# An encoder trunk on one core: how the gate, shift and scale rows of the conditioning are summed and turned

## The chip, the cores and the metric

The kernel runs on one core of a Trainium2 chip. The metric is device time in microseconds (us) of one execution. Several executions are given as a median with the lowest and highest.

## What is computed

Two layers, each of three sub-layers: a SwiGLU feed-forward block, a token mixer, a second SwiGLU block. Each sub-layer is conditioned by nine rows of 1024 numbers for a layer, three for each sub-layer (shift, scale, gate), which come from one vector c:

```python
for layer in range(DEPTH):                       # 2
    mod = (silu(c) @ w_ada[layer] + b_ada[layer]).reshape(b, N_SUB, 3, 1, D_MODEL)
    u = modulate(x, mod[:, 0, 0], mod[:, 0, 1])  # standardize(x) * (1 + scale) + shift
    f = swiglu(u, w_ffn_in[layer, 0], w_ffn_out[layer, 0])
    x = layer_norm(ALPHA * x + 0.5 * (1 + mod[:, 0, 2]) * f, ln_g[layer, 0], ln_b[layer, 0])
    # the mixer with mod[:, 1, :] (gate without the 0.5), the second SwiGLU with mod[:, 2, :]
```

x has 256 tokens of 1024 features; SwiGLU has 2816 hidden features. Everything is float32. w_ada is 1024 x 9216 for a layer.

## The kernel before

Tokens stand in two tiles of 128 partitions. A weight arrives by DMA as fp32 in a raw tile, is cast to fp32r by ACT (the high part, tiles h..) and subtracted from the raw tile by VectorE (the low part, tiles l..). A product of fp32 accuracy is then three fp32r products into the same PSUM bank (mm3, lines 150 to 153): high with high, high with low, low with high. In the trace ob and oa are the first products of a SwiGLU block, acc the second ones; ocx, ovx, ozx, oqkx and accx are those of the mixer.

All weights, the rows of w_ada among them, are items of one planned list (plan, step, issue_loads): the loads are issued in list order by SP as raw tiles come free (9 of them), and casts and splits take tiles from a pool of 26 (wtile). A SwiGLU block of 256 hidden features works in two halves j: 48 ob products, then 12 acc products of the block before (6 in the last blocks), then the evaluation of the half; after each half flush() emits what stands in the list late.

The conditioning goes like this. For each of the rows, ada_step (lines 318 to 333) takes eight raw tiles of 128 x 1024 and adds each, times a column of silu(c), into an accumulator of 128 x 1024 on VectorE. When the last one is in, ada_post (lines 386 to 406) is put in the list late. What remains to be done there is the sum over the 128 partitions:

- For a gate (w == 2) two fp32 products with a matrix of ones (pg, line 394) give the sum over the partitions on every partition, 512 columns each, and VectorE turns them into the gate's tile gr (line 395).
- For a shift or a scale four fp32 products with 32 columns of ones (pr, lines 398 to 400) each sum a quarter of the row, 256 columns, into one group of 32 partitions (tile_position). ACT copies that to SBUF (cpy, traced as adc), and two fp32 products with sel4 as the moving operand (pm, line 405) turn it into 8 columns, to which mod_cols (lines 375 to 384) adds the bias. sel4 (line 208) is 128 x 4 and has a one at partition 32 j of column j.

The first sub-layer's shift and scale go another way (adh_step) and are not touched. Ten rows go through the shift and scale branch, six through the gate branch. In the first SwiGLU block of layer 0 these are the mixer's shift and scale, the first gate, and the shift of the third sub-layer; in mixer 0 its gate and the scale of the third sub-layer; and so on, always before their use.

PSUM has a pool of two banks for small results (mps): pr, pg, pm and the transposes of the mixer (py) take turns in it. VectorE and ACT keep the written order in the transitions between sub-layers (cross, in_order); elsewhere the framework orders the instructions when the program is built, by their order in the program and by what is ready; TensorE is bound to the written order at the start of the program alone.

Of the kernel before, what the change touches and what calls it, by code (L numbers as in the profile page):

```python
# [12 lines left out]
F32R = mybir.dt.float32r  # L13
# [3 lines left out]
ALU = mybir.AluOpType  # L17
# [3 lines left out]
P = 128  # L21
D = 1024
KT = D // P
# [43 lines left out]
def kernel(  # L67
# [44 lines left out]
    V, S, PE = Queue(nc.vector), Queue(nc.scalar), Queue(nc.tensor)  # L112
# [9 lines left out]
    cp = ctx.enter_context(tc.tile_pool(name="cp", bufs=1))  # L122
# [9 lines left out]
    def wtile(shape, name, dt=F32):  # L132
        return wp.tile([P] + list(shape), dt, tag="w", name=name)

    def mps(name):
        return pms.tile([P, 512], F32, tag="ms", name=name)
# [10 lines left out]
    def f(ap):  # L147
        return ap.bitcast(F32)
# [6 lines left out]
    def split(src, hi, lo):  # L155
        S.copy(hi, src)
        V.tensor_tensor(lo, src, f(hi), op=ALU.subtract)


    ident = cp.tile([P, P], F32, name="ident")  # L160
    make_identity(nc, ident)
    ones = cp.tile([P, P], F32, name="ones")
# [29 lines left out]
    def issue_loads(upto):  # L192
        while pos["load"] < min(upto, 2 * len(items)):
            n = pos["load"]
            i, h = divmod(n, 2)
            kind, key, src = items[i]
            if kind == "pair":
                half = src[h].rearrange("(k p) c -> p k c", p=P)
            else:
                half = src.rearrange("(h k p) c -> h p k c", h=2, p=P)[h]  # L200
            shape = {"cols": [4, BC], "pair": [4, BC], "adh": [2, 512]}.get(kind, [1, D])
            raw = rp.tile([P] + shape, F32, tag="raw", name=f"raw_{key}_{h}")
            nc.sync.dma_start(raw, half)
            raws[n] = raw[:, 0, :] if shape[0] == 1 else raw
            pos["load"] += 1


    sel4 = cp.tile([P, 4], F32, name="sel4")
# [2 lines left out]
    sel1 = cp.tile([P, 1], F32, name="sel_all")  # L211
    V.tensor_reduce(sel1, sel4, axis=AX.X, op=ALU.add)

    ADA = ("ada", "adh")

    def hi_step():
        n = pos["hi"]
        i, h = divmod(n, 2)
        kind, key, _ = items[i]
        if kind in ADA:  # L220
            return False
# [13 lines left out]
    def step(n=1):  # L235
        for _ in range(n):
# [5 lines left out]
            issue_loads(k + 1)  # L242
            if kind in ADA:
                pos["hi"] = max(pos["hi"], k + 1)
# [35 lines left out]
    brs, bcol = [], []  # L280
# [26 lines left out]
    mods, gates, adas = {}, {}, {}  # L307
# [10 lines left out]
    def ada_step(key, raw, k):  # L318
        l, ch, q = key
        kt = 2 * q + k  # L320
        s, w = divmod(ch, 3)
        if kt == 0:
            adas[l, ch] = wtile([D], f"ada{l}_{ch}")
            if w == 2:
                G.memset(adas[l, ch], 0.0)
                nc.sync.dma_start(adas[l, ch][0:1, :], b_ada[l, ch * D:(ch + 1) * D].unsqueeze(0))
        acc = adas[l, ch]
        if kt == 0 and w < 2:
            keep(V.tensor_scalar(acc, raw, cT[:, 0:1], None, op0=ALU.mult), "v")
        else:  # L330
            keep(V.scalar_tensor_tensor(acc, raw, cT[:, kt:kt + 1], acc, op0=ALU.mult, op1=ALU.add), "v")
        if kt == KT - 1:
            late.append(lambda: ada_post(l, s, w, adas.pop((l, ch))))
# [41 lines left out]
    def mod_cols(l, s, w, pp):  # L375
        ch = 3 * s + w
        if w == 0:
            mods[l, s] = sm.tile([P, 2, KT], F32, tag="mod", name=f"mod{l}_{s}", bufs=3)
        md = mods[l, s]
        bc = bcol[l][:, ch * KT:(ch + 1) * KT]  # L380
        if w == 0:
            V.tensor_tensor(md[:, 0, :], pp[:, :KT], bc, op=ALU.add)
        else:
            V.scalar_tensor_tensor(md[:, 1, :], pp[:, :KT], 1.0, bc, op0=ALU.add, op1=ALU.add)

    def ada_post(l, s, w, acc):
        ch = 3 * s + w
        if w == 2:
            gr = wtile([D], f"gate{l}_{s}")
            gates[l, s] = gr  # L390
            half = 1.0 if s == 1 else 0.5
            for h in range(2):
                pp = mps(f"pg{l}_{s}_{h}")
                PE.matmul(pp, lhsT=ones, rhs=acc[:, h * 512:(h + 1) * 512], start=True, stop=True)
                V.tensor_scalar(gr[:, h * 512:(h + 1) * 512], pp, 1.0, half, op0=ALU.add, op1=ALU.mult)
            return
        pr = mps(f"pr{l}_{ch}")
        for j in range(4):
            PE.matmul(pr[32 * j:32 * j + 32, 0:256], lhsT=ones[:, 0:32], rhs=acc[:, j * 256:(j + 1) * 256],
                      start=True, stop=True, tile_position=(0, 32 * j))  # L400
        cpy = wtile([256], f"adc{l}_{ch}")
        S.copy(cpy, pr[:, 0:256])
        pp = mps(f"pm{l}_{ch}")
        for k in range(2):
            PE.matmul(pp[:, k:8:2], lhsT=cpy[:, k * P:(k + 1) * P], rhs=sel4, start=True, stop=True)
        mod_cols(l, s, w, pp)


    HALF = (slice(0, 512), slice(512, 1024))
# [949 lines left out]
```

## Time and profile before

| | |
|---|---|
| median of 3 runs | 1091.83 us (1090.25 to 1091.99) |
| profiled execution | 1089.88 us |
| its span, first to last instruction | 1088.2 us |
| mean granted TensorE clock | 0.986 of full speed |
| TensorE busy | 1041.0 us, 96% |
| VectorE busy | 834.7 us, 77% |
| ACT busy | 551.4 us, 51% |

PE is TensorE (its matrix products), PEld its loading of weights, DVE VectorE, ACT ScalarE, POOL GpSimd, SP the engine that issues the loads. In the rows "out<-in" names the tiles written and read; of a matrix product the moving operand comes first and the stationary one second. Durations of TensorE overlap, so what a product adds to the stream is read from the distance of starts, not from the durations. An fp32 product has two records, an fp32r product and a transpose one. "idle before <-" tells what ended the idle time of that engine. All rows that helpers record have the same line, L105.

### The profile page before, as it was taken

What the parts mean: (1) busy time and instruction counts of PE and PEld (TensorE: products, weight loads), DVE (VectorE), ACT (ScalarE), POOL (GpSimd) and SP (SyncE); (2) the same over time, 40 slices, a digit from 0 to 9 for tenths busy, and PEclk for the clock granted to TensorE, in tenths of its full rate; (3) what the DMA queues carried; (4) which work ended last, traced back from release to release, by engine and by line L of the source; (5) the groups of instructions that cost most, each with busy time, mean ns of one, the idle gap of its engine ahead of it and who ended that gap; (6) DMA issues with size and microseconds to landing.
All of it is one profiled execution on the core that took longest, in us unless ns stands there. A gap on an engine that the chain in (4) does not pass through costs nothing.

```text
span 1088.2 us, 18866 instructions
## 1 busy us (share of the span) xinstructions
PE 1041.0 (96%) x7381; PEld 953.2 (88%) x7381; DVE 834.7 (77%) x1303; ACT 551.4 (51%) x940; POOL 53.0 (5%) x93
## 2 busy tenths in 40 slices
PE   4999999999997999999999999999999989999996
PEld 2899999989895889999989999998989879999995
DVE  5788688589988898668589768756999888756454
ACT  3475344476654654334466434546566567435241
POOL 1000000020010200000020000000100120000000
PEclk9999999999999999999999999999999999999998
DMA  9989888838369389789737889784564638776411
GB/s 326 324 303 381 283 291 323 278 114 267 100 210 294 102 293 327 269 322 305 257 116 249 301 321 339 282 283 141 165 217 139 231 100 294 261 230 216 158 39 39
DMA packets 162557, 258.24 MB, mean 237 GB/s; under 512 B 10806, under 2 KB 125982, under 8 KB 162468
## 3 DMA queue, kind: packets, MB, share of 16 engines
q1 hardware_dynamic: 162468, 257.04, 69.9%
q8 instruction: 58, 0.95, 0.4%
q14 instruction: 31, 0.25, 0.1%
HBM read 255.96 MB, written 1.05 MB: 236 GB/s over the span
## 4 chain that ended last, share of the span: by engine, by line
PE 78%; DVE 9%; ACT 5%; DMA 4%; issue 3%; POOL 1%; SPq 0%; DVEq 0%; POOLq 0%; ACTq 0%
PE ob L105 38%; PE acc L105 20%; PE oqkx L105 4%; PE oa L105 4%; PE ocx L105 4%; PE accx L105 2%; DMA raw_g<-in_w_ffn_in_dram 1%; DVE ada L105 1%; PE ovx L105 1%; DVE xs L105 1%; ACT um L105 1%; DMA lb<-in_ln_b_dram 1%; DMA xs<-in_x_dram 1%; PE pg L105 1%; DVE accx L105 1%
## 5 line engine op out<-in xcount | busy, mean ns | idle before, releaser
L105 PE MATMUL ob<-uH,hg 128*128 128x256 f32 x576 | 164.5, 286 | 0.0
L105 PE MATMUL ob<-uL,hg 128*128 128x256 f32 x576 | 162.3, 282 | 0.0
L105 PE MATMUL ob<-uL,hu 128*128 128x256 f32 x576 | 161.8, 281 | 0.0
L105 PE MATMUL ob<-uH,lu 128*128 128x256 f32 x576 | 161.8, 281 | 0.0
L105 PE MATMUL ob<-uH,hu 128*128 128x256 f32 x576 | 161.8, 281 | 0.0
L105 PE MATMUL ob<-uH,lg 128*128 128x256 f32 x576 | 161.8, 281 | 0.0
L105 ACT ACTIVATE sgb<-ob 128x256 f32<-128x256 f32 x72 | 27.6, 384 | 227.2 <-PE ob L105 227.2
L105 PE MATMUL acc<-ho,hH 128*128 128x512 f32 x352 | 137.9, 393 | 1.3 <-ACT hH L105 1.3
L105 PE MATMUL acc<-lo,hH 128*128 128x512 f32 x352 | 138.1, 392 | 0.0
L105 PE MATMUL acc<-ho,hL 128*128 128x512 f32 x352 | 137.9, 393 | 0.0
L105 DVE TENSOR_TENSOR lo<-raw_o,ho 128x1024 fp32r<-128x1024 f32 x88 | 106.0, 1221 | 16.6 <-ACT ho L105 9.1
L105 PEld LDWEIGHTS ob<-uH,hg 128*128 128x128 f32 x576 | 108.3, 188 | 7.1 <-issue 4.4
L105 PEld LDWEIGHTS ob<-uL,hg 128*128 128x128 f32 x576 | 108.6, 188 | 3.3 <-issue 1.0
L105 DVE TENSOR_TENSOR lg<-raw_g,hg 128x1024 fp32r<-128x1024 f32 x84 | 100.7, 1221 | 11.7 <-ACT hg L105 5.1
L105 PEld LDWEIGHTS ob<-uL,hu 128*128 128x128 f32 x576 | 108.5, 188 | 0.0
L105 PEld LDWEIGHTS ob<-uH,lg 128*128 128x128 f32 x576 | 108.5, 188 | 0.1
L105 PEld LDWEIGHTS ob<-uH,hu 128*128 128x128 f32 x576 | 108.5, 188 | 0.0
L105 PEld LDWEIGHTS ob<-uH,lu 128*128 128x128 f32 x576 | 108.5, 188 | 0.0
L105 DVE TENSOR_TENSOR hfb<-ob,sgb 128x256 f32<-128x256 f32 x72 | 30.4, 422 | 99.2 <-ACT sgb L105 99.1
L105 DVE TENSOR_TENSOR lu<-raw_u,hu 128x1024 fp32r<-128x1024 f32 x84 | 100.3, 1219 | 4.9 <-ACT hu L105 2.9
L105 ACT CAST hg<-raw_g 128x1024 fp32r<-128x1024 f32 x84 | 86.4, 1050 | 31.5 <-DMA raw_g<-in_w_ffn_in_dram 16.5
L105 ACT CAST ho<-raw_o 128x1024 fp32r<-128x1024 f32 x88 | 90.2, 1048 | 11.4 <-PE ob L105 10.0
(534 smaller groups left out, 2259.3 us busy)
## 6 DMA issues: line engine op xcount, KB each, us to landing
raw_o<-in_w_ffn_out_dram SPq DMA_DIRECT2D x88, 512.0 KB, 6.7
raw_g<-in_w_ffn_in_dram SPq DMA_DIRECT2D x84, 512.0 KB, 5.8
raw_u<-in_w_ffn_in_dram SPq DMA_DIRECT2D x84, 512.0 KB, 6.8
raw<-in_w_ffn_in_dram SPq DMA_DIRECT2D x8, 512.0 KB, 8.8
lg<-in_ln_g_dram SPq DMA_DIRECT2D x6, 512.0 KB, 7.1
lb<-in_ln_b_dram SPq DMA_DIRECT2D x6, 512.0 KB
raw_qk0x<-in_w_in_dram SPq DMA_DIRECT2D x4, 512.0 KB, 8.6
raw_qk1x<-in_w_in_dram SPq DMA_DIRECT2D x4, 512.0 KB
```

Source lines behind the costliest of these rows:

```text
L105: ins = emit(*args, **kwargs)
```

## The change

Gate rows are now summed like shift and scale rows: the four narrow fp32 sums pr come first in ada_post for all three kinds. For a gate the result, 128 x 256 with the quarter j on partitions 32 j to 32 j + 31, is split into a high part (ACT, fp32r) and a low part (VectorE, fp32r) in a new tile adg of the pool of 26. Then eight fp32r products of 256 columns spread it: for each quarter j, first the high, then the low part as the moving operand, with column j of sel4r (a copy of sel4 in fp32r, made once), repeated 128 times, as the stationary one. So partition 32 j reaches all 128 partitions. The last step, by VectorE into gr, is as before.

For shift and scale the two fp32 products with sel4 give way to two fp32 transposes of 128 x 128 (cpy stationary, the identity moving). They write 256 columns of PSUM; mod_cols reads every 32nd of them.

```diff
+    sel4r = cp.tile([P, 4], F32R, name="sel4r")
+    V.tensor_copy(sel4r, sel4)
...
-        md = mods[l, s]
-        bc = bcol[l][:, ch * KT:(ch + 1) * KT]
+        md = mods[l, s][:, w, :].rearrange("p (j k) -> p j k", k=2)
+        bc = bcol[l][:, ch * KT:(ch + 1) * KT].rearrange("p (j k) -> p j k", k=2)
...
     def ada_post(l, s, w, acc):
+
         ch = 3 * s + w
+        pr = mps(f"pr{l}_{ch}")
+        for j in range(4):
+            PE.matmul(pr[32 * j:32 * j + 32, 0:256], lhsT=ones[:, 0:32], rhs=acc[:, j * 256:(j + 1) * 256],
+                      start=True, stop=True, tile_position=(0, 32 * j))
         if w == 2:
             gr = wtile([D], f"gate{l}_{s}")
             gates[l, s] = gr
             half = 1.0 if s == 1 else 0.5
+            cpy = wtile([2, 256], f"adg{l}_{ch}", F32R)
+            split(pr[:, 0:256], cpy[:, 0], cpy[:, 1])
             for h in range(2):
                 pp = mps(f"pg{l}_{s}_{h}")
-                PE.matmul(pp, lhsT=ones, rhs=acc[:, h * 512:(h + 1) * 512], start=True, stop=True)
+                for i in range(2):
+                    j = 2 * h + i
+                    for e in range(2):
+                        PE.matmul(pp[:, i * 256:(i + 1) * 256], lhsT=sel4r[:, j:j + 1].broadcast_to([P, P]),
+                                  rhs=cpy[:, e], start=(e == 0), stop=(e == 1))
                 V.tensor_scalar(gr[:, h * 512:(h + 1) * 512], pp, 1.0, half, op0=ALU.add, op1=ALU.mult)
             return
-        pr = mps(f"pr{l}_{ch}")
-        for j in range(4):
-            PE.matmul(pr[32 * j:32 * j + 32, 0:256], lhsT=ones[:, 0:32], rhs=acc[:, j * 256:(j + 1) * 256],
-                      start=True, stop=True, tile_position=(0, 32 * j))
         cpy = wtile([256], f"adc{l}_{ch}")
         S.copy(cpy, pr[:, 0:256])
         pp = mps(f"pm{l}_{ch}")
         for k in range(2):
-            PE.matmul(pp[:, k:8:2], lhsT=cpy[:, k * P:(k + 1) * P], rhs=sel4, start=True, stop=True)
-        mod_cols(l, s, w, pp)
+            PE.transpose(pp[:, k * P:(k + 1) * P], cpy[:, k * P:(k + 1) * P], ident)
+        mod_cols(l, s, w, pp[:, 0:256].rearrange("p (k j r) -> p j k r", k=2, j=4)[:, :, :, 0])
```

## Rows read from the trace of the kernel before

**Rows 1.** The page's chain that ended last: shares of the span by engine.
```profile
PE 78%; DVE 9%; ACT 5%; DMA 4%; issue 3%; POOL 1%; SPq 0%; DVEq 0%; POOLq 0%; ACTq 0%
```
**Rows 2.** Stretches: us; busy PE, PEld, DVE, ACT, POOL (instructions); clock, DMA, GB/s.
```profile
66.00:212.00 146.00, 146.00 (x1058) 135.17 (x1058) 114.71 (x129) 68.23 (x97) 0.95 (x1) 1.00 0.89 308
212.00:400.00 188.00, 174.85 (x1230) 158.09 (x1229) 166.33 (x329) 115.73 (x237) 20.31 (x30) 0.97 0.61 195
```
**Rows 3.** Waits of TensorE: who for whom; us in total, times, longest.
```profile
PE pg L105 <- DVE uL L105: 3.7, 1, 3.7
...
PE accx L105 <- ACT uH L105: 2.6, 3, 1.6
```
**Rows 4.** The chain in order of time: start, us, what; one run of ob products.
```profile
170.08 5.68 PE ob L105 x48
```
**Rows 5.** Tiles pr and pg: count; shortest, median, longest ns; first and last start.
```profile
L105 PE MATMUL pr<-ada,ones x80: 379/391/403, 98.1 to 717.4; 128*32 128x256 f32 x80
L105 ACT COPY adc<-pr x10: 372/372/374, 98.8 to 717.9; 128x256 f32<-128x256 f32 x10
...
L105 PE MATMUL pg<-ada,ones x24: 592/592/1222, 168.2 to 1036.7; 128*128 128x512 f32 x24
```
**Rows 6.** TensorE in order of time at a scale row (start us, us, engine, operation).
```profile
132.92 0.39 PE L105 MATMUL acc<-ho,hL 128*128 128x512 f32 x1
133.23 0.64 PE L105 MATMUL pr<-ada,ones 128*32 128x256 f32 x8
...
134.03 0.28 PE L105 MATMUL ob<-uL,hg 128*128 128x256 f32 x1
...
134.38 0.59 PE L105 MATMUL pm<-sel,adc 128*128 128x4 f32 x4
...
135.03 0.28 PE L105 MATMUL ob<-uH,lg 128*128 128x256 f32 x1
```
**Rows 7.** TensorE in order of time: two fp32 transposes among mixer products.
```profile
302.92 0.28 PE L105 MATMUL ovx<-lv1x,uH 128*128 128x256 f32 x1
303.04 0.38 PE L105 MATMUL pxsx<-ident,xcxx 128*128 128x128 f32 x2
303.18 0.37 PE L105 MATMUL ovx<-hv1x,uL 128*128 128x256 f32 x1
303.38 0.28 PE L105 MATMUL ovx<-hv1x,uH 128*128 128x256 f32 x1
```
**Rows 8.** All engines in order of time at the first gate, 166 to 178 us.
```profile
167.97 0.40 PE L105 MATMUL acc<-ho,hL 128*128 128x512 f32 x1
...
168.20 1.88 PE L105 MATMUL pg<-ada,ones 128*128 128x512 f32 x4
...
169.26 0.69 DVE L105 TENSOR_SCALAR gate<-pg 128x512 f32<-128x512 f32 x1 [1.83 <-PE pg L105]
...
170.04 0.28 PE L105 MATMUL ob<-uL,hg 128*128 128x256 f32 x1
...
170.73 2.35 DVE L105 TENSOR_TENSOR lg<-raw_g,hg 128x1024 fp32r<-128x1024 f32 x2
...
177.21 0.28 PE L105 MATMUL ob<-uH,lg 128*128 128x256 f32 x1
```
**Rows 9.** Groups of instructions: count; busy us, mean ns; idle before and releaser.
```profile
L105 DVE TENSOR_TENSOR hL<-ph,hH 128x256 fp32r<-128x256 f32 x16 | 6.4, 418 | 1.4 <-ACT hH L105 1.4
```
**Rows 10.** All engines in order of time in mixer 0, 338 to 352 us.
```profile
338.31 2.35 DVE L105 TENSOR_TENSOR lw1x<-raw_w1x,hw1x 128x1024 fp32r<-128x1024 f32 x2
...
340.58 1.28 DVE L105 TENSOR_SCALAR gate<-pg 128x512 f32<-128x512 f32 x2
...
341.32 0.64 PE L105 MATMUL pr<-ada,ones 128*32 128x256 f32 x8 [0.39 <-DVE gate L105]
...
342.72 0.38 SPq L477 DMA_DIRECT2D lb<-in_ln_b_dram  x1
...
351.00 1.06 ACT L105 ACTIVATE lb<-lb 128x1024 f32<-128x1024 f32 x1 [3.06 <-DMA lb<-in_ln_b_dram]
```

More of the change, by code (lines that the diff above doesn't have):

```diff
@@ L378, in mod_cols @@
             mods[l, s] = sm.tile([P, 2, KT], F32, tag="mod", name=f"mod{l}_{s}", bufs=3)
-        md = mods[l, s]
-        bc = bcol[l][:, ch * KT:(ch + 1) * KT]
+        md = mods[l, s][:, w, :].rearrange("p (j k) -> p j k", k=2)
+        bc = bcol[l][:, ch * KT:(ch + 1) * KT].rearrange("p (j k) -> p j k", k=2)
         if w == 0:
-            V.tensor_tensor(md[:, 0, :], pp[:, :KT], bc, op=ALU.add)
+            V.tensor_tensor(md, pp, bc, op=ALU.add)
         else:
-            V.scalar_tensor_tensor(md[:, 1, :], pp[:, :KT], 1.0, bc, op0=ALU.add, op1=ALU.add)
+            V.scalar_tensor_tensor(md, pp, 1.0, bc, op0=ALU.add, op1=ALU.add)
     def ada_post(l, s, w, acc):
         ch = 3 * s + w
+        pr = mps(f"pr{l}_{ch}")
+        for j in range(4):
+            PE.matmul(pr[32 * j:32 * j + 32, 0:256], lhsT=ones[:, 0:32], rhs=acc[:, j * 256:(j + 1) * 256],
+                      start=True, stop=True, tile_position=(0, 32 * j))
         if w == 2:
```

## The prediction

> **What bounds the kernel now.** I read four views, in this order. The chain of work that ended last puts 78% of the span on TensorE and 9% on VectorE [rows 1], so an edit counts above all by what it adds to TensorE's own queue. The table by stretches says where: in the first SwiGLU blocks (66 to 212 us) TensorE is busy for all 146 us at a granted clock of 1.00, the 2.4 GHz level, with VectorE at 115; in the stretch that holds mixer 0 (212 to 400) TensorE has 175 of 188 us and VectorE 166, so there VectorE's order can decide [rows 2]. TensorE's waits are few; the two that touch this change are in mixer 0, 3.7 us ahead of the gate's product and 1.6 us behind the reading of the lb row [rows 3]. Last I read the order of time around one place of each kind, because TensorE's durations overlap and only the distance of starts shows what a product costs the stream: 48 ordinary 256-column products take 5.68 us, 0.118 each [rows 4].
>
> There are ten shift or scale places (80 records of the sums, 8 each) and six gates (24 records, two products of two records each) [rows 5]. Nine of the ten lie inside SwiGLU blocks and one in mixer 0; four gates lie in SwiGLU blocks and one in each mixer.
>
> **Shift and scale columns.** Only the last step changes. Before: the sums start behind an acc product at 132.92, whose successor is due 0.23 later at 133.15, the second one at 133.27. The second ordinary product stands at 134.03, so the sums cost 0.76 us, and they stay. The column products (pm) start at 134.38, where the next ordinary one was due; the second ordinary one behind them is due at 134.50 and stands at 135.03, so they cost 0.53 [rows 5, 6]. In their place come two fp32 transposes of 128x128. The trace has such a pair in the middle of ordinary products: the second product behind it is due at 303.16 and stands at 303.38, 0.22 us [rows 7]. The gain is 0.53 - 0.22 = 0.31 us at each place. ACT's copy of 0.37 us and VectorE's small add stay. Nine places in an unbroken TensorE stream give 9 x 0.31 = 2.8 us. The tenth lies where VectorE decides; I count it at nothing there, with 0.3 at most.
>
> **Gate rows.** Removed: two fp32 products over 512 columns. They start at 168.20, just when an ordinary one was due; the second ordinary product is due at 168.32 and stands at 170.04, so a gate costs 1.72 us [rows 8]. Added: the four narrow sums, which are the very instructions of the shift places, 0.76 [rows 6]; and eight fp32r products of 256 columns at 0.118, 0.94 us [rows 4]. The sum is 1.70: the gate is even, 0.02 gained, 0.1 over the five gates outside mixer 0.
>
> The eight products have weights that repeat one column by a step of zero, and no row has such a load. From below it may cost nothing (the load lies under the product, as it does for ordinary ones); from above I take the nearest fp32 price, 0.43 us for 256 columns (half of a 512-column product, 1.72/4), which would add 0.31 x 8 = 2.5 us a gate. I take the fp32r price, because number format and column count are those of the ordinary rows.
>
> What the sums cost is where a rule speaks. The row shows 0.76 us for four sums, though their 256 columns at a quarter of a gate are 0.43. "TensorE: Matmul & The Clock Gate" of the Trainium skill, section Measured speedup vs the span model, has matmuls on separate column tiles run side by side, with about 4 ns more for each tile. By that the sums would cost 0.44 (an estimate from 0.43 and that figure) and each gate would gain 0.34, not 0.02. "TensorEngine Tiling", section Key Properties, has a change of tiling mode drain TensorE, which speaks against the change and is the side that the row takes: 0.33 us more than the columns.
>
> Beside TensorE each gate now needs an ACT copy (0.37, as adc [rows 5]) and a VectorE subtraction from PSUM (0.42 [rows 9]), and the products of low parts wait for both. Behind the waiting subtraction on VectorE stand the gate's own two rows of 0.69 and then the weight splits (lg). In the SwiGLU blocks that is covered: lg started at 170.73, and the product that reads its block stands at 177.21 [rows 8]; two casts and splits come between, so I put the cover at 4 us. I estimate 1.7 us from the first sum to the first low product (0.64 of sums, 0.37, 0.42, and some 0.1 for each handover), and lg about 1.1 us later than now. VectorE already sat idle for 1.83 us before the gate's row [rows 8], so the subtraction mostly fills a hole. If the cover were gone, each gate would cost those 1.1 us.
>
> TensorE's order is not kept strictly in these stretches; it is settled when the kernel is built. At the shift place the column products came four ordinary products behind the sums, and none was late [rows 6]. I take it that the low products are put some nine behind in the same way, and count no stall. The selection copy (sel4r) is one four-column VectorE instruction, made while the first x rows are still on their way: nothing, or 0.2 us without that cover. The gate's extra work tile adds no transfer. It takes one of 26 buffers for some 2 us; that can move a cast by a microsecond under the 4 us of cover: nothing.
>
> **Mixer 0** is the unknown cost. VectorE reads the gate's products at 340.58 behind its weight splits, the sums of the scale part wait for that (341.32), and the lg and lb loads for the buffers that these products free: lb goes out at 342.72, ACT waits for its landing until 351.00, and behind ACT stands a cast for which TensorE waits 1.6 us [rows 3, 10]. With the change a subtraction stands ahead of the gate rows: at least 0.42 us. If it takes the gate's old place, the products and their handover come behind it too: 0.42 + 0.5 + 0.2, about 1.2. From below: gates read between the splits, since their sums are done sooner, would send lb out early and give back at most 1.1 of the 1.6 us. I take 0.6, between 0.42 and 1.2, less what the queue ahead of lb (8.3 us from issue to landing) takes up. In mixer 1 VectorE also delays, but TensorE's work there goes on from other tiles: nothing.
>
> **The sum.** -2.8 - 0.1 + 0.6 = -2.3 us. The profiled execution took 1089.88 (span 1088.2 and 1.7 around it), which would be 1087.6. It is 1.95 below the median of the three runs, 1091.83; from that median the forecast is 1089.5. This is -0.21%, at the edge of what a measurement of this kernel can tell from no change, about 0.2% or 2.2 us.
>
> **The rivals.**
> First, the split's wait stalls TensorE. If no ordinary products stand between sums and spreading, TensorE waits for copy, subtraction and handovers, 1.1 us at each of five gates, 5.5 in all: 1091.83 - 2.9 + 5.5 + 0.6 = 1095.0, slower. It decides from fewer than nine ordinary products (1.1/0.118) in the gap. For it: TensorE does wait in its queue, 3.7 us for uL in mixer 0 [rows 3]. Against it: the four products so well placed at the shift places. Chance 0.15.
> Second, the sums pack side by side, or mixer 0 sends lb early. The first is 5 x 0.33 = 1.6 better, 1087.9; the second 0.6 + 1.1 = 1.7 better, 1087.8. Against the first stand ten places at 0.76; for the second that the gate's sums end sooner. By the span rule of the skill the first is the time to expect; the trace disagrees with it by 0.33 us a place. Chance 0.17 together.
> Third, the gain is lost at the borders of the stages, where VectorE and loads, not TensorE, set the next start, or mixer 0 loses 2 us and more: 1091.3 to 1092. For it: VectorE's 166 of 188 us [rows 2]. Against it: the waits of TensorE are few. Chance 0.2.
> Fourth, the repeated-column load goes at the fp32 price: 5 x 2.5 = 12 more, 1102. No row speaks for it. Chance 0.03.
> The forecast, 1089.5 within a microsecond, has 0.45.
>
> **How the numbers follow.** The forecast lies at the edge, so I split its 0.45 into 0.28 below 1089.65 and 0.17 above. Faster: 0.28 + 0.17 = 0.45. The same: 0.17 + 0.2 = 0.37. Slower: 0.15 + 0.03 = 0.18. The range leaves the slow cases out (0.18) and takes in the two better cases and the third with their bounds: 1086.9 (a microsecond below 1087.9) to 1093.0 (a microsecond above 1092).
>
> **What would show it.** Right: pairs of transposes with the second ordinary product 0.22 us late, at nine places; gates at 1.70, with ordinary products between the sums and the eight; no TensorE wait on the subtraction. Wrong: a TensorE wait ended by a VectorE split of the gate; spreading products more than 0.118 apart; lb in mixer 0 issued more than 1.2 us later against the chain before it, or earlier; other stretches that grow or shrink by more than these terms because the build put instructions elsewhere.

## The result: 1080.6 us, a percent faster, and most of it not from the change's operations

| | before | after |
|---|---|---|
| median (lowest to highest), us | 1091.60 (1090.25 to 1091.99), 4 runs | 1080.62 (1079.14 to 1082.18), 4 runs |
| profiled execution, us | 1089.88 | 1082.18 |
| its span, us | 1088.2 | 1080.3 |
| TensorE busy, us | 1041.0 | 1035.6 |

The ratio is 0.9905 with a 95% interval of 0.9893 to 0.9917. The forecast was 1089.5 with a range of 1086.9 to 1093.0: the direction was right, and the time lies 6.3 us below the range. The two traces stand 7.9 us apart, less than the medians (the profiled execution of after is the slowest of its four); shares in this section are of the 7.9.

First the places where the change is. In TensorE's order of time at the scale row, the kernel after:

```profile
132.44 0.39 PE L105 MATMUL acc<-ho,hL 128*128 128x512 f32 x1
132.76 0.64 PE L105 MATMUL pr<-ada,ones 128*32 128x256 f32 x8
...
133.55 0.28 PE L105 MATMUL ob<-uL,hg 128*128 128x256 f32 x1
...
133.78 0.28 PE L105 MATMUL ob<-uH,hg 128*128 128x256 f32 x1
133.90 0.42 PE L105 MATMUL pm<-ident,adc 128*128 128x128 f32 x2
...
134.28 0.28 PE L105 MATMUL ob<-uH,lg 128*128 128x256 f32 x1
```

Against [rows 6]: the transposes start when an ordinary product was due, at 133.90; the second one behind them is due at 134.02 and stands at 134.28. The pair costs 0.26, where the prediction had 0.22 from the mixer's row [rows 7] and the fp32 products cost 0.53. By the same count all nine places in SwiGLU blocks have 0.26, so the gain is 0.27 at each, 2.4 us.

All engines but the weight loads (PEld) at the first gate, the kernel after (the bracket gives idle time ahead and who ended it):

```profile
167.01 0.39 PE L105 MATMUL acc<-ho,hL 128*128 128x512 f32 x1
167.32 0.64 PE L105 MATMUL pr<-ada,ones 128*32 128x256 f32 x8
167.89 0.39 PE L105 MATMUL ob<-uH,hg 128*128 128x256 f32 x1
168.03 0.37 ACT L105 CAST adg<-pr 128x256 fp32r<-128x256 f32 x1 [1.98 <-PE pr L105]
168.12 0.28 PE L105 MATMUL ob<-uL,hg 128*128 128x256 f32 x1
...
168.35 0.28 PE L105 MATMUL ob<-uH,hg 128*128 128x256 f32 x1
168.43 0.42 DVE L105 TENSOR_TENSOR adg<-pr,adg 128x256 fp32r<-128x256 f32 x1 [1.92 <-ACT adg L105]
168.47 0.37 PE L105 MATMUL pg<-adg,sel4r 128*128 128x256 f32 x1
168.68 0.28 PE L105 MATMUL ob<-uL,hg 128*128 128x256 f32 x1
...
169.04 0.28 PE L105 MATMUL ob<-uL,hg 128*128 128x256 f32 x1
169.15 0.98 PE L105 MATMUL pg<-adg,sel4r 128*128 128x256 f32 x7
169.70 1.29 DVE L105 TENSOR_SCALAR gate<-pg 128x512 f32<-128x512 f32 x2 [0.84 <-PE pg L105]
169.97 0.28 PE L105 MATMUL ob<-uH,lg 128*128 128x256 f32 x1
```

The sums cost 0.76 again: the second product behind them is due at 167.01 + 0.23 + 0.12 = 167.36 and stands at 168.12. The first spreading product adds 0.21 (168.35 to 168.68 is 0.33, less 0.12), the other seven 0.81 (169.04 to 169.97, less 0.12). That is 1.78 for a gate, where [rows 8] gave 1.72: the gate is even to 0.06. The other three gates in SwiGLU blocks have the same. TensorE waits for nothing here; four ordinary products stand behind the sums and four more behind the first high product.

So far all is close to what was foreseen. The difference stands where nothing was changed. The chain that ended last, in order of time (start, us, what), 72 to 90 us, well ahead of the first row whose sums or columns the change touches (98 us), shows two halves j of the first SwiGLU block. Before:

```profile
72.84 5.68 PE ob L105 x48
78.52 2.77 PE acc L105 x12
81.28 5.68 PE ob L105 x48
```

After:

```profile
73.14 5.65 PE ob L105 x48
78.80 2.72 PE acc L105 x12
81.52 5.65 PE ob L105 x48
```

A half takes 8.37 us in place of 8.44, with the same instructions. 62 runs of 48 ob products in the trace of before have 118.28 ns a product and more, none less; 58 in that of after have 117.8 or less. Of the mixer's first products the same view has a run of 34, before and then after:

```profile
284.58 4.04 PE ocx L105 x34
```

```profile
282.59 3.89 PE ocx L105 x34
```

From the mean distance of starts of neighbouring products of one tile: ob 118.28 to 117.59 ns (3349 of them), acc 229.64 to 227.42 (957), ocx 118.36 to 114.99 (356), accx 233.08 to 229.46 (170); oa rises from 116.78 to 117.29 (680), and three more of the mixer rise too: oqkx from 117.07 to 117.66 (338), ozx from 116.75 to 117.70 (178), ovx from 116.92 to 117.10 (170). The sum of these is 2.3 + 2.1 + 1.2 + 0.6 - 0.3 - 0.4 = 5.5 us of the 7.9.

### The profile page after: what moved, and what is told of

Read it like the earlier page. It is cut to its first block, busy times and chain, and to the rows that moved or that the text cites. A ratio compares the mean times of both kernels' runs of the same rounds, so it can differ in the third digit from the quotient of the medians.

```text
span 1080.3 us, 18994 instructions
## 1 busy us (share of the span) xinstructions
PE 1035.6 (96%) x7433; PEld 950.9 (88%) x7433; DVE 835.1 (77%) x1310; ACT 553.1 (51%) x946; POOL 53.0 (5%) x93
## 3 DMA queue, kind: packets, MB, share of 16 engines
HBM read 255.96 MB, written 1.05 MB: 238 GB/s over the span
## 4 chain that ended last, share of the span: by engine, by line
PE 77%; DVE 11%; ACT 6%; DMA 2%; issue 2%; POOL 1%; SPq 0%; DVEq 0%; POOLq 0%; ACTq 0%
PE ob L105 37%; PE acc L105 18%; PE oa L105 6%; PE oqkx L105 5%; PE accx L105 3%; PE ocx L105 2%; DVE xs L105 1%; PE ovx L105 1%; DVE ada L105 1%; DVE acc L105 1%; DVE cax L105 1%; PE pr L105 1%; ACT um L105 1%; ACT junk L105 1%; DVE lu L105 1%
## 5 line engine op out<-in xcount | busy, mean ns | idle before, releaser
L105 DVE TENSOR_TENSOR lu<-raw_u,hu 128x1024 fp32r<-128x1024 f32 x84 | 100.6, 1220 | 3.5 <-ACT hu L105 1.9
L105 ACT CAST hg<-raw_g 128x1024 fp32r<-128x1024 f32 x84 | 86.3, 1050 | 32.0 <-PE acc L105 18.2
```

Of the source, the lines that this page charges most:

```text
L105: ins = emit(*args, **kwargs)
```

## The experiments

What could reach products that the change does not touch? The instructions in these stretches are the same, and the durations of VectorE's and ACT's instructions beside them are too (a weight split 1220 ns in both traces, a cast 1050). What differs is the place of the tiles in on-chip memory. The new tile sel4r takes 32 bytes per partition, and every tile that is allocated behind it moves by 32. The compiled programs give the places; they are not in the profile. The table below holds them in bytes modulo 128, with what the chain between 70 and 92 us shows of each kernel. Tiles u are the moving operand of ob and ocx and the stationary one of oa; the weight tiles are the other operand of each; h is the stationary operand of acc. In the built programs the instructions of each engine stand in one order in before, e1, e2, e9 and e11, and in one order in after, e3, e7, e8, e10 and e12, but for the one or two small copies that fill an added tile.

| kernel | u | weights | raw | h | ob x48, us | half, us | ratio to before |
|---|---|---|---|---|---|---|---|
| before | 64 | 96 | 96 | 96 | 5.68 | 8.44 | 1 |
| after | 64 | 0 | 0 | 0 | 5.65 | 8.37 | 0.9905 |
| e1_pad32 | 64 | 0 | 0 | 0 | 5.65 | 8.37 | 0.9924 |
| e2_pad64 | 64 | 32 | 32 | 32 | 5.70 | 8.44 | 1.0022 |
| e3_after_old_places | 64 | 96 | 96 | 96 | 5.68 | 8.45 | 0.9971 |
| e4_transposes_only | 64 | 96 | 96 | 96 | 5.68 | 8.45 | 0.9979 |
| e5_gates_only | 64 | 96 | 96 | 96 | 5.68 | 8.45 | 0.9993 |
| e6_transposes_pad32 | 64 | 0 | 0 | 0 | 5.65 | 8.37 | 0.9905 |
| e7_after_wp_only | 64 | 0 | 32 | 32 | 5.46 | 8.25 | 0.9874 |
| e8_after_pad96 | 64 | 64 | 64 | 64 | 5.76 | 8.52 | 1.0045 |
| e9_hp_only | 64 | 96 | 96 | 0 | 5.68 | 8.48 | 1.0018 |
| e10_raw_only_off | 64 | 0 | 32 | 0 | 5.45 or 5.65 | 8.23 or 8.42 | 0.9909 |
| e11_u_only | 32 | 96 | 96 | 96 | 5.65 | 8.37 | 0.9930 |
| e12_pad96_u64 | 0 | 64 | 64 | 64 | 5.65 | 8.37 | 0.9930 |

The first expectations call the ob products down products and the acc products up products; it is the other way round, ob are the first ones of a block.

**e1_pad32: the tile alone.**

```diff
     V.tensor_reduce(sel1, sel4, axis=AX.X, op=ALU.add)
+    sel4r = cp.tile([P, 4], F32R, name="sel4r")
+    V.tensor_copy(sel4r, sel4)
```

> The kernel before with nothing but the added four-column tile of the selection matrix and its one copy; no product of the change is in it. Theory (places): this tile moves every later tile of the on-chip memory by 32 bytes per partition, and TensorE reads its operands at a steadier cadence from the new places: the runs of 48 SwiGLU down products take 117.8 ns per product in place of 118.3, the 512-column products of the up stage 227.4 in place of 229.6, and the time is 4 to 6 us below before, 1086 to 1087.5. Rival (the change's own operations bring all of it, through the order of the work): the cadence stays at 118.3 and 229.6 and the time at 1091.6.

Measured: 0.9924 (0.9909 to 0.9939), 8.3 us less than before, of the 10.4 that 0.9905 stands for. The chain of this kernel:

```profile
74.21 5.65 PE ob L105 x48
79.86 2.72 PE acc L105 x12
82.58 5.65 PE ob L105 x48
```

It is the cadence of after, from a four-column tile that nothing in this kernel reads. The theory of places stands; that the change's operations bring all of the gain falls. The effect is larger than the 4 to 6 us expected: in this trace the mixer's ocx and accx products give 2.0 us (114.49 and 229.61 ns), and the mean of ob falls to 117.07, under the 117.8 of the runs of 48.

**e2_pad64: the same tile, 64 bytes long** (`cp.tile([P, 16], ...)`, the copy into its first four columns).

> The kernel before with an added tile of 16 columns, which moves every later tile by 64 bytes in place of 32, so that the weights, hidden rows and row tiles start 32 bytes past a multiple of 64 as they do in the kernel before. Theory (places, by the remainder modulo 64): no change, 118.3 ns per down product and 1091.6 us. Rival (any shift of the places, or one more tile and copy, does it): 117.8 ns and 1086 to 1087.5.

Measured: 1.0022 (1.0012 to 1.0032), 2.4 us slower. So an added tile and copy are not what helps. But "no change" was not right either: ob went to 118.54 and oa from 116.78 to 119.84 ns.

```profile
72.62 5.70 PE ob L105 x48
```

The remainder modulo 64, which this kernel keeps, is not the whole rule.

**e3_after_old_places: the whole change without the move.** sel4 and sel1 share one tile, which frees the 32 bytes.

```diff
-    sel4 = cp.tile([P, 4], F32, name="sel4")
+    sel8 = cp.tile([P, 8], F32, name="sel8")
+    sel4, sel1 = sel8[:, 0:4], sel8[:, 4:5]
...
-    sel1 = cp.tile([P, 1], F32, name="sel_all")
```

> The whole change, with the two old selection tiles packed into one, so that all later tiles lie exactly where they lie in the kernel before. Theory (places): down products go back to 118.3 ns, up products to 229.6, and the kernel loses 4 to 6 us of the change's gain: 1085 to 1088, which is what the change's operations are worth alone (forecast 1089.5). Rival (the operations bring it all): 1080.6 and 117.8 ns.

Measured: 0.9971 (0.9962 to 0.9981), 3.2 us less than before, 2.1 to 4.1; that is 7.2 us above the whole change, more than the 4 to 6 expected. The cadence is that of before:

```profile
74.41 5.68 PE ob L105 x48
80.09 2.77 PE acc L105 x12
82.86 5.68 PE ob L105 x48
```

So the operations of the change are worth 3.2 us, where the prediction's sum had 2.3, and this kernel is the one that the prediction described. With e1 the two parts give 0.76% + 0.29% = 1.05%, and the whole change has 0.95% (0.83 to 1.07): they add within the noise.

**e4_transposes_only** (the change in mod_cols and in the last loop of ada_post alone, old places).

> The kernel before with the shift and scale columns made by transposes and all else as before, at the old places. By the forecast's term for it: nine places at 0.31 us, -2.8 us, 1088.8, and a cadence of 118.3 ns. Rival (gain lost at the stage borders): 1091 to 1091.6. Rival (transposes also change the cadence): 1084 or less with 117.8 ns.

Measured: 0.9979 (0.9969 to 0.9989), 2.3 us, 1.2 to 3.4, where the term was 2.8.

**e5_gates_only** (sums, split and spreading for the gates, columns by fp32 products, old places by the shared tile of e3).

> The gates' part of the change alone (sums, split, eight spreading products), columns as before, and the two old selection tiles packed into one so that all later tiles lie where they lie in the kernel before. By the forecast's term: -0.1 for five gates and about +0.6 or nothing in mixer 0, so within 1 us of before (ratio 0.999 to 1.001), ob at 118.3. Rival (the gates carry part of the gain): 1 to 2 us faster.

Measured: 0.9993 (0.9984 to 1.0003), within the noise, as expected. Together e4 and e5 give 0.28%, and e3 has 0.29%. In the trace of e5 the stretch from the first accx to the next block's first oa product in mixer 0 takes 41.57 us, in that of before 40.93: +0.64, beside the +0.6 that the prediction took for mixer 0. But in e11, which changes no instruction there, this stretch is 42.76, so one trace doesn't carry a term of this size. The traces differ in TensorE's mean granted clock there as well: 0.96 of full speed in before, 0.87 or 0.88 in all others.

**e6_transposes_pad32** (e4 with the tile of e1): is the gates' part needed?

> Transposes for the shift and scale columns, gates as before, and the added four-column tile with its copy, which moves all later tiles to multiples of 64 bytes. If the two effects add: the tile alone gave -0.76% (8.3 us) and the transposes alone -0.21% (2.3 us), so -0.97%, about 1081 against 1091.6, level with the whole change, and ob products at 117.1 to 117.6 ns. If the gates' part carried something of its own that only shows at the new places: 1 us or more above the whole change. If they overlap (both take out the same irregular products): -0.8%.

Measured: 0.9905 (0.989 to 0.992), level with the whole change. Transposes and one unused tile are as good as all of it.

**e7_after_wp_only: which tiles matter.** The whole change, and a pool of 32 unused bytes behind the weight tiles.

```diff
     wp = ctx.enter_context(tc.tile_pool(name="wp", bufs=NW))
+    gp = ctx.enter_context(tc.tile_pool(name="gp", bufs=1))
     rp = ctx.enter_context(tc.tile_pool(name="rp", bufs=NRAW))
...
+    gap = gp.tile([P, 8], F32, name="gap")
+    V.tensor_copy(gap[:, 0:4], sel4)
```

> The whole change, with 32 unused bytes behind the pool of weight tiles: these stay at multiples of 64 bytes, while raw tiles, the hidden rows (h) and the row tiles go back to 32 bytes past such a multiple. Theory (the weights' place matters as moving and as stationary operand): ob 117.1 to 117.6 ns, acc 227.4, accx 229.5, time as the whole change, 0.9905 of before. Rival (for acc the stationary h rows matter): ob 117.1 to 117.6, but acc 229.6, and the time 2.2 us (957 acc products by 2.3 ns) above the whole change, 0.9925.

Measured: 0.9874 (0.9859 to 0.9889), the fastest kernel of all, 13.7 us below before. Neither side had that:

```profile
73.58 5.46 PE ob L105 x48
79.04 2.79 PE acc L105 x12
81.83 5.46 PE ob L105 x48
```

acc became slower, as the rival said and by more (232.85 ns), but the ob runs dropped to 113.5 ns. Three runs of 48 at 113.5 to 113.7 stand in the trace of after as well (205, 719 and 913 us); so these weights' places allow two cadences of ob, 117.8 and 113.5, and the stream changes between them. In e7 54 of its 58 runs go at 113.5 to 113.9.

**e9_hp_only: the hidden rows alone moved**, by a gap of 32 bytes ahead of their pool in the kernel before.

> The kernel before with 32 unused bytes ahead of the pool of hidden rows: weights and raw tiles stay at 32 bytes past a multiple of 64, the hidden rows (h) and row tiles go to multiples of 64. Theory (the weights' place matters): ob 118.3, acc 229.6, time as before. Rival (acc's stationary h rows matter): ob 118.3, acc 227.4, time 2.2 us below before.

Measured: 1.0018 (1.0006 to 1.0030). ob stayed (118.32), acc went the wrong way for both theories, to 233.34 ns. In e7 and e9, where h and the weights of acc have different remainders modulo 64, acc takes 233; where they have the same one it takes 227 to 230 (e10 is the exception, below).

**e8_after_pad96: 64 bytes further than after.**

> The whole change with one more selection tile of 16 columns: all later tiles 64 bytes further on, still at multiples of 64, but 64 bytes past a multiple of 128, where the whole change has multiples of 128. If only the remainder modulo 64 counts: ob 117.1 to 117.6, acc 227.4, ratio to before 0.9905. If 128 counts: ob and acc as before (118.3, 229.6), 0.997; or oa, oqkx and ozx at 119.9 in place of 117, as in the kernel with 64 added bytes, which would cost 1370 products by 2.9 ns, 4 us, 0.994.

Measured: 1.0045 (1.0028 to 1.0062), with the whole change in it 4.9 us slower than before. So the remainder modulo 128 counts, but neither of the two times given for that (0.997 and 0.994) came: ob itself went to 119.85 ns in most runs of 48.

```profile
74.49 5.76 PE ob L105 x48
80.25 2.76 PE acc L105 x12
83.01 5.76 PE ob L105 x48
```

**e10_raw_only_off: why e7 is faster.** Gaps of 32 and 96 bytes around the raw tiles' pool.

> The whole change with two unused gaps: weights, hidden rows (h) and row tiles at multiples of 128 bytes, as in the whole change, the raw tiles alone 32 bytes past such a multiple. It tells why the kernel with weights at 128 and all the rest 32 bytes past it had ob at 113.5 (and acc at 232.9). If the hidden rows set both, through the acc products that run between the ob runs: as the whole change, ob 117.8, acc 227.4, 0.9905. If the raw tiles, which the casts and splits read, set ob: ob 113.5 and acc 227.4, 12 us below before plus 5 us for acc, 0.983.

Measured: 0.9909 (0.9890 to 0.9927), the time of the whole change, but not with its cadence. Of its 58 ob runs 24 go at about 113.5 and 34 at 117.8, most often in turns:

```profile
71.82 5.45 PE ob L105 x48
77.27 2.77 PE acc L105 x12
80.05 5.65 PE ob L105 x48
```

and acc takes 231.60 ns although h and the weights have one remainder. Against the trace of after ob gives back 4.8 us and acc costs 4.0, so the time stays. Neither account holds. The kernels e10 and after differ by the raw tiles' place and two unused gaps with their copies, so the raw tiles' place matters for which cadence TensorE falls into, though the ob products don't read them. ACT and VectorE do, and the loads write them. How they act on TensorE stays open.

**e11_u_only: is it the weights' place, or their distance from u?** The kernel before, with neghalf, the tile ahead of x and u, 96 bytes longer, and the 32-byte tile of e1 behind u, so that all others move by 128.

```diff
-    neghalf = cp.tile([P, 16], F32, name="neghalf")
+    neghalf = cp.tile([P, 40], F32, name="neghalf")
```

> The kernel before with the two u tiles (and x) alone moved, by 96 bytes; weights, raw tiles, hidden rows and row tiles keep their remainder of 96 bytes past a multiple of 128. The weights are then 64 bytes past u, modulo 128, as in the whole change. If the distance of the two operands counts: ob 117.8 and ocx 114.5, as in the whole change, acc at 229.6 or 227.4, and at least 3 us (3350 ob and ocx products by 0.5 to 4 ns) below before. If the weights' own place counts: ob 118.3, ocx 118.4, time as before.

Measured: 0.9930 (0.9910 to 0.9950), 7.6 us less than before, without one operation of the change:

```profile
74.39 5.65 PE ob L105 x48
80.04 2.72 PE acc L105 x12
82.76 5.65 PE ob L105 x48
```

ocx fell to 114.49 as in e1. The weights kept their remainder; u alone moved, and with it its distance to them. acc, whose operands have not moved against each other, went to 227.29 too. It runs between ob runs, and here its cadence went with theirs; e9, with 233.3 beside an unchanged ob, shows that theirs alone doesn't set it.

**e12_pad96_u64: the same question at the slow end.** Weights, raw tiles and h exactly where e8 has them, u 64 bytes further on (neghalf `[P, 32]` in the whole change).

> The whole change with weights, raw tiles, hidden rows and row tiles at exactly the places of the slowest kernel so far (the one with 96 added bytes, 1.0045 of before), but with the u tiles 64 bytes further on as well, so that the weights lie 64 bytes past u, modulo 128, in place of 0. If the distance of weights and u sets the cadence: ob back to 117.8 and ocx to 114.5, half periods of 8.37 in place of 8.52 us, ratio about 0.990. If the weights' own place counts: ob 119.9, ocx 118.6, ratio 1.0045.

Measured: 0.9930 (0.9907 to 0.9953), against 1.0045 for e8:

```profile
73.94 5.65 PE ob L105 x48
79.59 2.72 PE acc L105 x12
82.31 5.65 PE ob L105 x48
```

1.15%, some 12 us, comes back by moving the moving operand's tiles by 64 bytes. By the distance of the weights from u, modulo 128, ob runs of 48 take 5.76 us at 0 (e8), 5.68 at 32 (before, e3 to e5, e9), 5.65 or 5.46 at 64 (after, e1, e6, e7, e10 to e12) and 5.70 at 96 (e2). The distance of 64 was tried at three places of u (64, 32 and 0); those of 0, 32 and 96 at one each, so that it is the distance and not the places is shown for 64 alone. That it is the weights' distance, and not that of h or raw, follows from e7, where only the weights stand 64 from u, and e9, where only h does.

## Why the prediction was wrong

**The step that failed** is the sentence on the selection copy: "one four-column VectorE instruction, made while the first x rows are still on their way: nothing, or 0.2 us without that cover". As an instruction that is right: its row in the trace of after has 160 ns at 2.3 us. But the edit is a tile as well as an instruction, and I priced only the instruction. The tile moves all that is allocated behind it, and that was worth 8.3 of 10.4 us (e1). No rival covered it either. The last item of "what would show it", stretches that change by more than the terms, did happen, but the cause named there, another order of instructions, is not the one: e1 has the order of before and after's cadence.

**The steps that held, but for one term.** Shift and scale: -2.8 foreseen, -2.3 (-3.4 to -1.2) measured by e4; the term was a little too large, since a pair of transposes costs 0.26 among ob products, not the 0.22 of the mixer's row. The sum: -2.3 foreseen, -3.2 (-4.1 to -2.1) by e3. The gates in SwiGLU blocks: 0.02 cheaper foreseen, 0.06 dearer in the trace. With the +0.6 for mixer 0 the gates' part was to cost 0.5; e5 has -0.8 (-1.7 to +0.3), so that +0.6 did not show. The rivals at the places did not come: no wait for the split, none of the spreading products at the fp32 price (0.116 each for the seven), the sums at 0.76 and not side by side. By the span rule of the Trainium skill, "TensorE: Matmul & The Clock Gate", section Measured speedup vs the span model, the sums would have taken 0.44 (the prediction's estimate); the trace of after has 0.76 at a gate too.

**Mixer 0** was read wrongly in two places, and what they come to is not resolved: its stretch from the first accx to the next block's first oa product takes 41.10 us in after and 40.93 in before, at unlike mean granted clocks (0.88 and 0.96, see e5). All engines in order of time, the kernel after:

```profile
338.89 0.42 DVE L105 TENSOR_TENSOR adg<-pr,adg 128x256 fp32r<-128x256 f32 x1
...
340.15 0.38 SPq L487 DMA_DIRECT2D lb<-in_ln_b_dram  x1
...
340.64 0.98 PE L105 MATMUL pg<-adg,sel4r 128*128 128x256 f32 x7
341.19 1.29 DVE L105 TENSOR_SCALAR gate<-pg 128x512 f32<-128x512 f32 x2 [1.28 <-PE pg L105]
...
347.79 1.06 ACT L105 ACTIVATE lb<-lb 128x1024 f32<-128x1024 f32 x1
```

The mixer's accx products start 2.0 us earlier than before here. The gate's rows on VectorE start 0.61 later than in [rows 10], so 2.6 later against the stream, where I allowed 1.2. But lb went out 2.6 earlier by the clock and 0.5 against the stream: it is issued ahead of these rows (340.15 against 341.19), where before it came behind them. The sum had it go out later; lb sent early was half of the second rival, so that half came, without the shorter stretch that it was priced at. ACT reads lb without a wait, and the wait that it passed on is smaller. The waits of TensorE in after, to be read beside [rows 3]:

```profile
PE pr L105 <- DVE uL L105: 3.0, 1, 3.0
...
PE accx L105 <- ACT uH L105: 1.2, 3, 0.8
```

## What to carry to other kernels

An added tile is an edit of the memory map: before pricing a change, list which tiles move, and against which operand. To know what an edit's operations are worth, time it with all later tiles at their old places (here by packing two small tiles into one), and time the move alone; here the first gives 0.3% and the second 0.8%, and a 32-byte gap elsewhere another 0.3%. Where products stand at a cadence that is the same to the nanosecond in nearly every run (118.3 in 58 of the 62 in before), compare it between the two kernels ahead of the first touched place: that comparison led to the cause.

## What the runs showed of the hardware

Not expected: TensorE's cadence goes with the byte distance of its two operands' tiles in a partition. With the same 256-column fp32r products (ob, runs of 48) at a granted clock of 1.00 most runs take 119.85, 118.28, 117.77 or 118.70 ns a product at distances of 0, 32, 64 and 96 bytes modulo 128, and at 64 some take 113.53. Between the worst and the best of these kernels (e8 and e7, which hold the same instructions apart from one small copy each) lie 1.7% of the time.

Open is by what mechanism the distance acts; what sets the choice between 117.8 and 113.5 ns, which depends on the places of tiles that these products don't read (e10); and why acc takes 227 in some kernels and 230 to 233 in others. The cadence terms, 5.5 us, and the change's own 3.2 by e3 make 8.7, between the 7.9 of the two traces and the 10.4 of the medians; the parts add up no better than that.
